# RMS norm factors by columns: two float32r matmuls with ones, root and reciprocal behind them, in a one-core decoder layer

## The chip, the cores and the metric

The kernel runs on one core of one Trainium2 chip. The metric is the device time of one execution in microseconds (us). The kernel before was timed three times. One further execution was taken with the hardware profiler; all rows of the profile come from that execution, and their times count from the start of its span.

The core has five engines with queues of their own that run in order: TensorE (PE in the profile, its weight loads are PEld), VectorE (DVE), ScalarE (ACT), GpSimd (POOL) and SyncE (SP), which issues most transfers. `te`, `ve`, `se` and `ge` stand for the first four in the code. PSUM has 8 banks of 128 x 512 float32 here, which take the results of matmuls.

## The reference

One layer of a decoder over 1024 prompt tokens and 8 x 4 decode tokens, model width 1024, in float32. Cut to what matters:

```
def _rms(x, g):
    return x * rsqrt(mean(x * x, axis=-1) + EPS) * g

h = _rms(x, n_mix_pre);  z = h @ w_in              # q, k, v, pooling input u
m = concat(attention(q, k, v), pool(u)) @ w_out
x = x + _rms(m, n_mix_post)
f = _rms(x, n_ffn_pre)
f = (silu(f @ w_gate) * (f @ w_up)) @ w_down
x = x + _rms(f, n_ffn_post)
x = x + sigmoid(x @ w_ple_gate) * (p @ w_ple)
```

The attention has 8 query heads on 2 key heads of 64, a window of 128 keys, and a learned sink for each head. The decode tokens attend to a cache of 128 keys for each of 8 sequences and to their own 4 keys. There are four norms on the way of every token.

## The kernel before

**Layout.** Activations are kept with channels on the 128 partitions and tokens along the columns. The 1056 tokens are cut into three groups of 352 columns (`G`, `N`); group 2 holds the last prompt tokens and the decode tokens. A matrix product of float32 is made of three float32r matmuls: each operand is split into a rounded part `hi` (a cast on ACT) and the rest `lo` (a subtraction on DVE, lines 157 and 160 in `split`), and `gemm` issues hi x hi, hi x lo and lo x hi. Nearly all of PE's work is matmuls of 128x128 weights with 352 columns, recorded at one line (126, in the helper `mm`).

**Stages.** In order of the span: the pooling input's projections with the first norm (to about 57 us), keys, values and queries (to about 135), the decode and prompt attention mixed with parts of the output projection (136 to 240), the rest of the output projection with the norms around the residual (240 to 285), the FFN (285 to 1010; group 2 goes ahead with five slabs of the hidden dimension alone, and groups 0 and 1 share products by sums of weights that POOL makes), and the per-layer input with its gate (to the end).

**The norms.** A norm's sum runs over channels, which lie on partitions and in eight column blocks. The blocks' squares are first added into one tile `acc` of 128 x 352 (`sum_halves`, `squares_into`). `rstd_steps(acc)` then makes the factor 1/sqrt(mean + eps) for each token. It is called twelve times: once for each group in front of the projections (`u_norm`, whose factor is used by `u_evict` and when keys, values and queries leave PSUM), twice for each group in `ffn_steps` (the norm behind the mixing, consumer line 834, and that in front of the FFN, line 846), and once for each group in `ple_steps` (consumer line 1050). Before, the four quarters of `acc`, 88 tokens each, are the stationary side of four narrow float32 matmuls with a column of ones; this gives sums with tokens on 88 partitions and four columns. Root (line 295), reciprocal (296) and split (298, 299) run on that 88x4 tile. Two products with the identity (line 303) spread the two parts over diagonals `dg`, and two float32r matmuls of ones with `dg` bring the factor back to all 128 partitions, in PSUM, where the consumers read it.

**What sets the order.** PE's instructions are pinned to the order of the program. Those of DVE and ACT are placed by a scheduler. `chain` and `turn` are a planner for the side work: a chain is a generator that yields (load, wait), in units of one 352-column matmul; `turn(n)` adds n units of PE time after a product and runs the chains whose time has come, where the time grows by load over a share (0.6, later 0.45, 0.1 and 0.7) plus the wait. So the two numbers that `rstd_steps` yields set how many matmuls of other work are between its two halves. For the three norms in front the two halves are placed by hand, with `u_norm`.

**The weights.** They are loaded by SP three tiles ahead and split when the program comes to them, so casts (ACT) and subtractions (DVE) of weights stand in the same queues as the norms.

**Decode attention.** `dscores(kv)` makes scores of 128 rows by 1056 keys for one key head, in three matmuls whose two operands lie on one half of the partitions (64 rows), adds the mask (line 688) and calls `softmax` (lines 589 to 603, the last step on POOL). `dturned` transposes the result block by block into a tile, and `dvalues(kv, pt, o)` multiplies nine blocks with the cached values, into one half of the output's partitions (64 columns of weights). Each of the nine matmuls takes all 128 columns, although for one cached sequence only 16 of them are not zero.

**The end.** `ple_out` makes two products for one block of channels and one group: `pp` from the per-layer input (2 blocks deep, 6 matmuls) and `pg` for the gate (8 deep, 24 matmuls), then sigmoid, multiplication, addition and the store.

Of the kernel before, what the change touches and what calls it, by code (L numbers as in the profile page):

```python
# [25 lines left out]
N = T // G  # L26
# [4 lines left out]
TB = 4  # L31
# [30 lines left out]
def trunk_kernel(  # L62
# [32 lines left out]
    te, ve, se, ge = nc.tensor, nc.vector, nc.scalar, nc.gpsimd  # L95
# [4 lines left out]
    spool = ctx.enter_context(tc.tile_pool(name="spool", bufs=2))  # L100
# [23 lines left out]
    def mm(*args, **kw):  # L124

        ins = te.matmul(*args, **kw)  # L126
        if pinned[0]:
            tc.keep_in_program_order(ins)

    def bank():  # L130
        return psum.tile([P, 512], F32, tag="b", name=nm("b"))

    def tmp(n, s="t", dt=F32):
        return spool.tile([P, n], dt, tag="tmp", bufs=6, name=nm(s), padded_shape=[P, NX])
# [21 lines left out]
    def split(hi, lo, src):  # L156
        ins = se.copy(hi, src)  # L157
        if not pairs:
            tc.keep_in_program_order(ins)
        ve.tensor_tensor(lo, src, hi.bitcast(F32), op=ALU.subtract)  # L160
# [124 lines left out]
    def rstd_steps(acc):  # L285

        n = acc.shape[1]
        w = n // TB  # L290
        sm = bank()
        for i in range(TB):
            mm(sm[:w, i : i + 1], acc[:, i * w : (i + 1) * w], ones[:, 0:1], start=True, stop=True)
        sd = spool.tile([P, TB], F32, tag="sd", name=nm("sd"))
        se.activation(sd[:w], sm[:w, :TB], AF.Sqrt, bias=epst[:w], scale=1.0 / D)
        ve.reciprocal(sd[:w], sd[:w])
        hl = spool.tile([P, 2, TB], F32R, tag="hl", name=nm("hl"))
        ve.tensor_copy(hl[:w, 0], sd[:w])
        ve.tensor_tensor(hl[:w, 1], sd[:w], hl[:w, 0].bitcast(F32), op=ALU.subtract)
        dgs = []  # L300
        for h in range(2):
            dg = tmp(n, "dg", F32R)
            ve.tensor_tensor(
                dg[:w].rearrange("p (i k) -> p i k", k=w),
                ident[:w, :w].unsqueeze(1).to_broadcast([w, TB, w]),
                hl[:w, h].bitcast(F32).unsqueeze(2).to_broadcast([w, TB, w]),
                op=ALU.mult,
            )
            dgs.append(dg)
        yield 6, 14  # L310
        ps = bank()
        for h in range(2):
            mm(ps[:, :n], ones_r[:w, :], dgs[h][:w], start=h == 0, stop=h == 1)
        return ps[:, :n]

    def acc_tile(g):
        return spool.tile([P, NS[g]], F32, tag=f"acc{g}", bufs=1, name=nm("acc"))
# [32 lines left out]
    xs, acc1, r1 = [[None] * 2 for _ in range(G)], [None] * G, [None] * G  # L350
# [51 lines left out]
    n = 4 * NDEC * PST  # L402
# [44 lines left out]
    def u_norm(steps, g):  # L447
        try:
            next(steps)
        except StopIteration as e:  # L450
            se.copy(acc1[g], e.value)
            r1[g] = acc1[g]

    pinned[0] = True
    norms = [None] * G
# [70 lines left out]
    for i, j in enumerate([WK, WV, *WQ]):  # L526
        w = weights(j)
# [3 lines left out]
        for g in range(G):  # L531
            ps = bank()
# [6 lines left out]
    kT, vT, qT = qkv[0], qkv[1], qkv[2:]  # L539
# [12 lines left out]
    skp, skd = const([P, 8], sink_p), const([P, 2], sink_d)  # L552
    nskp, nskd = const([P, 8]), const([P, 2])
# [32 lines left out]
    def softmax(t, nh, scale, sk, nsk):  # L586

        mx = spool.tile([P, nh], F32, tag="mx", name=nm("mx"))
        ve.tensor_reduce(mx, t, axis=AX.X, op=ALU.max)  # L589
        nmx = spool.tile([P, nh], F32, tag="nmx", name=nm("nmx"))  # L590
        ve.scalar_tensor_tensor(nmx, mx, -scale, nsk, op0=ALU.mult, op1=ALU.min)
        es = spool.tile([P, nh], F32, tag="es", name=nm("es"))
        ve.tensor_tensor(es, sk, nmx, op=ALU.add)
        se.activation(es, es, AF.Exp)
        sm = spool.tile([P, nh], F32, tag="sm", name=nm("sm"))
        for c in range(nh):
            se.activation(  # L597
                t[:, c, :], t[:, c, :], AF.Exp, bias=nmx[:, c : c + 1], scale=scale, accum_out=sm[:, c : c + 1]
            )
        ve.tensor_tensor(sm, sm, es, op=ALU.add)  # L600
        ve.reciprocal(sm, sm)
        nk = t.shape[2]
        ge.tensor_tensor(t, t, sm.unsqueeze(2).to_broadcast([P, nh, nk]), op=ALU.mult)  # L603
# [70 lines left out]
    nc.sync.dma_start(dmt, dmask)  # L674
    NK = NDEC * WIN + NDEC * DSEQ

    def dscores(kv):
        rows = slice(64 * kv, 64 * kv + 64)
        q = qd[rows]
        t = act_tile([P, 1, NK])  # L680
        for lo, n in ((0, 512), (512, 512), (1024, NDEC * DSEQ)):
            ps = bank()
            if lo < 1024:
                k = ckt[rows].rearrange("p b w -> p (b w)")[:, lo : lo + n]
            else:
                k = kT[rows, SEQ:]
            mm(ps[:, :n], q, k, start=True, stop=True)
            ve.tensor_tensor(t[:, 0, lo : lo + n], ps[:, :n], dmt[:, lo : lo + n], op=ALU.add)
        softmax(t, 1, 0.125, skd[:, kv : kv + 1], nskd[:, kv : kv + 1])
        return t  # L690

    def dturned(t):
        pt = act_tile([P, NDEC + 1, P])
        for lo in (0, 4, 8):
            ps = bank()
            n = min(4, NDEC + 1 - lo)
            if lo < 8:
                for i in range(n):
                    mt(ps[:, i * P : (i + 1) * P], t[:, 0, (lo + i) * P : (lo + i + 1) * P])
                se.copy(pt[:, lo : lo + n, :], ps.rearrange("p (b c) -> p b c", c=P))  # L700
            else:
                mt(ps[: NDEC * DSEQ, :P], t[:, 0, 1024:])
                se.copy(pt[: NDEC * DSEQ, 8, :], ps[: NDEC * DSEQ, :P])
        return pt

    def dvalues(kv, pt, o):
        cols = slice(64 * kv, 64 * kv + 64)
        for b in range(NDEC):
            mm(o[cols, :P], cvt[:, b, cols], pt[:, b, :], start=b == 0, stop=False)
        mm(o[cols, :P], vdec[:, cols], pt[: NDEC * DSEQ, 8, :], start=False, stop=True)  # L710

    def out_pool(m, g):

# [47 lines left out]

    order = [5, 6, 7, 0, 1, 2, 3, 4]
    pinned[0] = True
    td = [dscores(kv) for kv in range(2)]
    t = scores(order[0])
    filler(2)
    od = bank()
    pt0 = dturned(td[0])
    filler(1)
    pt1 = dturned(td[1])  # L770
    dvalues(0, pt0, od)
    filler(1)
    dvalues(1, pt1, od)
    put(od, SEQ, NDEC * DSEQ)
    kse = act_tile([P, NDEC, WIN])
    ge.tensor_copy(kse[:, :, : WIN - DSEQ], ckt[:, :, DSEQ:])
# [4 lines left out]
    for a, b in zip(order, order[1:] + [None]):  # L781
# [5 lines left out]
        t = t2  # L787
# [300 lines left out]
    def ple_out(n, m, g):  # L1088
        ph, pl = pls[g]
        w = WPE[n][m]  # L1090
        wh, wl = need(w[0])
        cols = slice((m % 4) * P, (m % 4 + 1) * P)
        pp, pg = bank(), bank()
        gemm(pp[:, :N], [(wh[:, k, cols], wl[:, k, cols], ph[:, k, :], pl[:, k, :]) for k in range(2)])
        gemm(pg[:, :N], ops8(need(w[1]), x2s[g]))
        turn(30)
        sg = tmp(N, "sg")
        se.activation(sg, pg[:, :N], AF.Sigmoid)
        xm = x2[g][m // 4][:, m % 4, :]
        ve.tensor_tensor(sg, sg, pp[:, :N], op=ALU.mult)  # L1100
        yo = tmp(N, "yo")
        ve.tensor_tensor(yo, sg, xm, op=ALU.add)
        nc.sync.dma_start(y_o[:, m, OFF[g] : OFF[g + 1]], yo)
# [105 lines left out]
```

## Time and profile before

| | |
|---|---|
| time, median of 3 runs | 1135.78 us (1133.85 to 1135.8) |
| the profiled execution's own time | 1133.7 us |
| its span | 1131.9 us |
| its granted TensorE clock, mean | 0.998 |
| PE busy | 1119.0 us (99%) |
| DVE, ACT, POOL busy | 745.5, 440.4, 176.0 us |
| read from memory, written | 88.30 MB, 10.11 MB |

How to read it: a group's row names line, engine, operation, output <- inputs, partitions x elements and count, then busy time, mean ns of one, and the idle time of the engine just ahead with what ended it. A row of the timeline gives start and duration, and in brackets the idle time ahead and what ended it. Neighbours of one kind are put into one row with a count. PE's matmuls overlap in its pipeline: one of 352 columns lasts some 323 ns in the records, and the next starts 160 ns after it.

### The profile page before, as it was taken

The page shows a single profiled execution, that of the slowest core. Times are in us where ns is not written, and L with a number is a line of the kernel's source. Part 1 is how long each engine was busy: PE and PEld are TensorE (multiplying, and loading weights), DVE is VectorE, ACT ScalarE, POOL GpSimd, SP SyncE. Part 2 cuts the span into 40 slices and gives each one's busy share as a digit, 9 for nine tenths or more (in the row PEclk, how much of TensorE's full clock was granted, in tenths as well). Part 3 has the DMA queues.
Part 4 walks back from the last instruction along what each step waited for, and adds up shares of the span by engine and source line. Part 5 has one row for each costly group of instructions (what it writes and reads, how often), then busy time and mean ns, then how long its engine had stood idle before and what let it go on. Part 6 is the DMA issues. An engine that isn't in the chain of part 4 may idle for free.

```text
span 1131.9 us, 17571 instructions
## 1 busy us (share of the span) xinstructions
PE 1119.0 (99%) x7119; PEld 1096.0 (97%) x7119; DVE 745.5 (66%) x1234; ACT 440.4 (39%) x772; POOL 176.0 (16%) x149
## 2 busy tenths in 40 slices
PE   8999999999999999999999999999999999999998
PEld 8999988699999999999999999999999999999998
DVE  7567357876888965256555555557887876789532
ACT  8223266754555533332221313123434334366220
POOL 0045032200000032111110201111123123100000
PEclk9999999999999999999999999999999999999999
DMA  8121301172454312112020211211322222256211
GB/s 285 49 77 39 126 37 38 39 268 85 172 192 131 112 56 75 38 39 75 25 70 19 75 38 41 73 38 60 119 73 76 75 75 75 85 172 213 89 59 39
DMA packets 34689, 99.54 MB, mean 88 GB/s; under 512 B 4116, under 2 KB 14644, under 8 KB 34608
## 3 DMA queue, kind: packets, MB, share of 16 engines
q1 hardware_dynamic: 32848, 96.65, 25.5%
q10 hardware_dynamic: 1760, 1.78, 0.5%
q8 instruction: 56, 0.92, 0.3%
q14 instruction: 25, 0.20, 0.1%
HBM read 88.30 MB, written 10.11 MB: 87 GB/s over the span
## 4 chain that ended last, share of the span: by engine, by line
PE 90%; DVE 5%; ACT 3%; issue 1%; DMA 1%; POOL 1%; DVEq 0%; POOLq 0%; ACTq 0%
PE b L126 89%; ACT a L597 1%; DVE mx L589 1%; DVE wl L160 1%; ACT wh L157 1%; PE b L120 1%; DMA wr<-in_w_in_dram 1%; POOL wr L923 0%; DVE a L634 0%; DVE h L360 0%; ACT h L357 0%; DMA c<-in_gains_dram 0%; DVE o L1050 0%; DVE x L1054 0%; POOL a L603 0%
## 5 line engine op out<-in xcount | busy, mean ns | idle before, releaser
L126 PE MATMUL b<-fh,wh 128*128 128x352 f32 x808 | 260.6, 323 | 0.0
L126 PE MATMUL b<-fh,wl 128*128 128x352 f32 x808 | 260.6, 323 | 0.0
L126 PE MATMUL b<-fl,wh 128*128 128x352 f32 x808 | 259.5, 321 | 0.0
L126 PE MATMUL b<-hid,wh 128*128 128x352 f32 x1056 | 253.6, 322 | 1.7 <-DVE o L1050 1.2
L157 ACT CAST wh<-wr 128x1024 fp32r<-128x1024 f32 x137 | 143.5, 1049 | 263.5 <-PE b L126 227.5
L160 DVE TENSOR_TENSOR wl<-wr,wh 128x1024 fp32r<-128x1024 f32 x137 | 171.2, 1252 | 64.6 <-ACT wh L157 64.3
L126 PEld LDWEIGHTS b<-hid,wh 128*128 128x128 f32 x1056 | 183.5, 188 | 2.5 <-issue 1.5
L126 PE MATMUL b<-hid,wl 128*128 128x352 f32 x528 | 170.1, 322 | 0.0
L923 POOL TENSOR_TENSOR wr<-wr 128x512 f32<-128x512 f32 x44 | 63.5, 1443 | 630.5 <-DVE wl L160 454.6
L126 PEld LDWEIGHTS b<-fh,wl 128*128 128x128 f32 x808 | 152.9, 189 | 0.0
L126 PEld LDWEIGHTS b<-fl,wh 128*128 128x128 f32 x808 | 151.9, 188 | 0.0
L126 PEld LDWEIGHTS b<-fh,wh 128*128 128x128 f32 x808 | 151.5, 188 | 0.0
L1020 DVE TENSOR_TENSOR o<-o,b 128x352 f32<-128x352 f32 x240 | 114.6, 515 | 27.4 <-PE b L126 27.0
L126 PE MATMUL b<-fh,sh 128*128 128x352 f32 x352 | 113.6, 323 | 0.0
L126 PE MATMUL b<-fh,sl 128*128 128x352 f32 x352 | 113.4, 322 | 0.0
L126 PE MATMUL b<-fl,sh 128*128 128x352 f32 x352 | 113.0, 321 | 0.0
L126 PE MATMUL b<-h,wh 128*128 128x352 f32 x480 | 105.9, 326 | 1.4 <-ACT h L357 0.9
L160 DVE TENSOR_TENSOR sl<-wr,sh 128x1024 fp32r<-128x1024 f32 x44 | 53.8, 1222 | 75.1 <-ACT sh L157 75.1
L126 PEld LDWEIGHTS b<-hid,wl 128*128 128x128 f32 x528 | 99.8, 189 | 0.0
L157 ACT CAST sh<-wr 128x1024 fp32r<-128x1024 f32 x44 | 45.7, 1047 | 131.3 <-POOL wr L923 91.0
L126 PEld LDWEIGHTS b<-h,wh 128*128 128x128 f32 x480 | 82.3, 190 | 2.7 <-ACT h L357 1.4
L126 PEld LDWEIGHTS b<-fh,sl 128*128 128x128 f32 x352 | 66.5, 189 | 0.0
(150 smaller groups left out, 1594.9 us busy)
## 6 DMA issues: line engine op xcount, KB each, us to landing
wr<-in_w_gu_dram SPq DMA_DIRECT2D x64, 512.0 KB, 3.3
wr<-in_w_dn_dram SPq DMA_DIRECT2D x32, 512.0 KB, 3.4
wr<-in_w_pg_dram SPq DMA_DIRECT2D x14, 512.0 KB, 3.8
wr<-in_w_in_dram SPq DMA_DIRECT2D x10, 512.0 KB, 4.2
x<-in_x_dram SPq DMA_DIRECT2D x6, 704.0 KB, 11.1
x1d<-x SPq DMA_DIRECT2D x6, 704.0 KB, 3.6
x<-x1d SPq DMA_DIRECT2D x6, 704.0 KB, 5.8
out_y_dram<-yo SPq DMA_DIRECT2D x24, 176.0 KB, 1.8
```

The lines of the kernel that those rows point to most:

```text
L120: ins = te.transpose(out, src, ident)
L126: ins = te.matmul(*args, **kw)
L157: ins = se.copy(hi, src)
L160: ve.tensor_tensor(lo, src, hi.bitcast(F32), op=ALU.subtract)
L589: ve.tensor_reduce(mx, t, axis=AX.X, op=ALU.max)
L597: se.activation(t[:, c, :], t[:, c, :], AF.Exp, bias=nmx[:, c : c + 1], scale=scale, accum_out=sm[:, c : c + 1])
L923: ge.tensor_tensor(out, a, b, op=op)
L1020: ve.tensor_tensor(o, o, v, op=ALU.add)
```

## The change

It has three parts.

1. `rstd_steps`: the narrow matmuls, the root and reciprocal on 88x4, and the diagonals go. `acc` itself is split into two float32r tiles, `ah` and `al`, and two float32r matmuls with a 128x128 tile of ones give each token's sum on all partitions. Root and reciprocal are made there on 128x352, from PSUM into `acc` (in SBUF), which is the factor. The yield between the two halves becomes (4, 8) instead of (6, 14). `u_norm` no longer copies the factor out of PSUM.
2. Decode: `dscores` makes the scores of both key heads, alternating between them, and calls both softmaxes behind. `dvalues` makes both heads' values in one block: the new keys' matmul first, over all 128 columns, and then one matmul for each sequence and head, alternating, over the 16 columns (4 heads x 4 tokens) that belong to that sequence.
3. `ple_out`: the gate's product is issued first, its sigmoid next, and then the product of the per-layer input.

```
     def rstd_steps(acc):
         n = acc.shape[1]
-        w = n // TB
-        sm = bank()
-        for i in range(TB):
-            mm(sm[:w, i : i + 1], acc[:, i * w : (i + 1) * w], ones[:, 0:1], start=True, stop=True)
-        sd = spool.tile([P, TB], F32, tag="sd", name=nm("sd"))
-        se.activation(sd[:w], sm[:w, :TB], AF.Sqrt, bias=epst[:w], scale=1.0 / D)
-        ve.reciprocal(sd[:w], sd[:w])
...
-        for h in range(2):
-            dg = tmp(n, "dg", F32R)
-            ve.tensor_tensor(
...
-        yield 6, 14
+        hi, lo = tmp(n, "ah", F32R), tmp(n, "al", F32R)
+        split(hi, lo, acc)
+        yield 4, 8
         ps = bank()
-        for h in range(2):
-            mm(ps[:, :n], ones_r[:w, :], dgs[h][:w], start=h == 0, stop=h == 1)
-        return ps[:, :n]
+        mm(ps[:, :n], ones_r, hi, start=True, stop=False)
+        mm(ps[:, :n], ones_r, lo, start=False, stop=True)
+        se.activation(acc, ps[:, :n], AF.Sqrt, bias=epst, scale=1.0 / D)
+        ve.reciprocal(acc, acc)
+        return acc
...
         except StopIteration as e:
-            se.copy(acc1[g], e.value)
-            r1[g] = acc1[g]
+            r1[g] = e.value
...
-    def dscores(kv):
-        rows = slice(64 * kv, 64 * kv + 64)
...
+    def dscores():
+        ts = [act_tile([P, 1, NK]) for _ in range(2)]
         for lo, n in ((0, 512), (512, 512), (1024, NDEC * DSEQ)):
+            for kv in range(2):
+                rows = slice(64 * kv, 64 * kv + 64)
...
+                mm(ps[:, :n], qd[rows], k, start=True, stop=True)
+                ve.tensor_tensor(ts[kv][:, 0, lo : lo + n], ps[:, :n], dmt[:, lo : lo + n], op=ALU.add)
+        for kv in range(2):
+            softmax(ts[kv], 1, 0.125, skd[:, kv : kv + 1], nskd[:, kv : kv + 1])
+        return ts
...
-    def dvalues(kv, pt, o):
-        cols = slice(64 * kv, 64 * kv + 64)
+    def dvalues(pts, o):
+        sides = [slice(64 * kv, 64 * kv + 64) for kv in range(2)]
+        def own(a, b):
+            return a.rearrange("p (h r) -> p h r", h=4)[:, :, DSEQ * b : DSEQ * (b + 1)]
+        for pt, cols in zip(pts, sides):
+            mm(o[cols, :P], vdec[:, cols], pt[: NDEC * DSEQ, 8, :], start=True, stop=False)
         for b in range(NDEC):
-            mm(o[cols, :P], cvt[:, b, cols], pt[:, b, :], start=b == 0, stop=False)
-        mm(o[cols, :P], vdec[:, cols], pt[: NDEC * DSEQ, 8, :], start=False, stop=True)
+            for pt, cols in zip(pts, sides):
+                mm(own(o[cols, :P], b), cvt[:, b, cols], own(pt[:, b, :], b), start=False, stop=b == NDEC - 1)
...
-    td = [dscores(kv) for kv in range(2)]
+    td = dscores()
     t = scores(order[0])
     filler(2)
     od = bank()
-    pt0 = dturned(td[0])
+    pts = [dturned(td[0])]
     filler(1)
-    pt1 = dturned(td[1])
-    dvalues(0, pt0, od)
+    pts.append(dturned(td[1]))
     filler(1)
-    dvalues(1, pt1, od)
+    dvalues(pts, od)
...
-        gemm(pp[:, :N], [(wh[:, k, cols], wl[:, k, cols], ph[:, k, :], pl[:, k, :]) for k in range(2)])
         gemm(pg[:, :N], ops8(need(w[1]), x2s[g]))
-        turn(30)
         sg = tmp(N, "sg")
         se.activation(sg, pg[:, :N], AF.Sigmoid)
+        gemm(pp[:, :N], [(wh[:, k, cols], wl[:, k, cols], ph[:, k, :], pl[:, k, :]) for k in range(2)])
+        turn(30)
```

More of the change, by code (lines that the diff above doesn't have):

```diff
@@ L289, in rstd_steps @@
         n = acc.shape[1]
-        w = n // TB
-        sm = bank()
-        for i in range(TB):
-            mm(sm[:w, i : i + 1], acc[:, i * w : (i + 1) * w], ones[:, 0:1], start=True, stop=True)
-        sd = spool.tile([P, TB], F32, tag="sd", name=nm("sd"))
-        se.activation(sd[:w], sm[:w, :TB], AF.Sqrt, bias=epst[:w], scale=1.0 / D)
-        ve.reciprocal(sd[:w], sd[:w])
[L297 to L300, printed above, removed]
-        for h in range(2):
-            dg = tmp(n, "dg", F32R)
[L303 to L309, printed above, removed]
-        yield 6, 14
-        ps = bank()
-        for h in range(2):
-            mm(ps[:, :n], ones_r[:w, :], dgs[h][:w], start=h == 0, stop=h == 1)
-        return ps[:, :n]
+        hi, lo = tmp(n, "ah", F32R), tmp(n, "al", F32R)
+        split(hi, lo, acc)
+        yield 4, 8
+        ps = bank()
+        mm(ps[:, :n], ones_r, hi, start=True, stop=False)
[3 more added lines that the diff above has]
+        return acc
     def acc_tile(g):
@@ L675, in trunk_kernel @@
     NK = NDEC * WIN + NDEC * DSEQ
-    def dscores(kv):
-        rows = slice(64 * kv, 64 * kv + 64)
-        q = qd[rows]
-        t = act_tile([P, 1, NK])
+    def dscores():
+        ts = [act_tile([P, 1, NK]) for _ in range(2)]
         for lo, n in ((0, 512), (512, 512), (1024, NDEC * DSEQ)):
[L682 to L690, printed above, removed]
+            for kv in range(2):
+                rows = slice(64 * kv, 64 * kv + 64)
+                ps = bank()
+                if lo < 1024:
+                    k = ckt[rows].rearrange("p b w -> p (b w)")[:, lo : lo + n]
+                else:
+                    k = kT[rows, SEQ:]
+                mm(ps[:, :n], qd[rows], k, start=True, stop=True)
[3 more added lines that the diff above has]
+        return ts
     def dturned(t):
```

## The prediction

> **What bounds the kernel now.** I read the busy times first, then the chain of work that ended last, then the list of what TensorE (PE) waited for, then stage windows, and last the timelines around the places that the change touches.
>
> ```profile
> span 1131.9 us, 17571 instructions
> PE 1119.0 (99%) x7119; PEld 1096.0 (97%) x7119; DVE 745.5 (66%) x1234; ACT 440.4 (39%) x772; POOL 176.0 (16%) x149
> PE 90%; DVE 5%; ACT 3%; issue 1%; DMA 1%; POOL 1%; DVEq 0%; POOLq 0%; ACTq 0%
> ...
> PE b L126 <- DVE dg L303: 2.0, 2, 1.6
> PE b L126 <- DVE o L1050: 1.2, 1, 1.2
> PE b L126 <- DVE hid L160: 0.5, 1, 0.5
> ...
> 300.00:420.00 120.00, 120.00 (x761) 119.96 (x760) 102.00 (x135) 60.69 (x74) 8.44 (x4) 1.00 0.41 139
> ```
>
> PE is busy for 99% of the span and is 90% of the chain that ended last. The waits row reads "PE waited for DVE's tile dg 2.0 us in all, 2 times, at most 1.6". In the window from 300 to 420 us (columns: length, then PE, weight loads, DVE, ACT and POOL busy with their counts, clock, DMA share, GB/s) PE has no idle time and the clock is 1.00. So what counts is the work on PE itself, to the last tenth of a microsecond, and whatever makes PE wait that did not before. DVE's 66% and ACT's 39% are cover, except where they sit between two PE instructions.
>
> **Part 1: the norm without its turn to columns.** Twelve norms run through the changed helper: one for each of 3 groups ahead of the projections, two for each in the mixing and FFN norms, one for each before the per-layer input.
>
> ```profile
> 24.77 0.71 PE L126 MATMUL b<-c,acc 128*88 128x1 f32 x8
> ...
> 26.71 0.80 PE L126 MATMUL b<-h,wl 128*128 128x352 f32 x4
> 29.11 0.78 PE L126 MATMUL b<-dg,c 88*128 88x352 f32 x2 [1.60 <-DVE dg L303]
> 31.65 1.44 PE L126 MATMUL b<-h,wh 128*128 128x352 f32 x8
> 32.93 0.81 PE L126 MATMUL b<-h,wl 128*128 128x352 f32 x4
> ...
> L126 PE MATMUL b<-c,acc 128*88 128x1 f32 x96 | 8.5, 211 | 0.0
> L126 PE MATMUL b<-dg,c 88*128 88x352 f32 x24 | 6.4, 344 | 2.2 <-DVE dg L303 2.0
> ```
>
> The 96 passes of the four narrow float32 matmuls (8 a norm) go. Rows overlap in PE's pipeline, so I take the spacing, not the duration: with them, from the start of the passes to the start of the next 4 matmuls of the same block is 26.71 - 24.77 = 1.94 us; the same block without them takes 32.93 - 31.65 = 1.28. That is 0.66 a norm, 12 x 0.66 = **-7.9 us** of PE work. The two wide matmuls stay: 24 before, with the diagonals dg, 24 after, with the squares' halves as the moving side. Same 352 columns, same type, so I count no difference.
>
> The first norm makes PE wait 1.60 us for dg. Four matmuls in a row take 0.81 (at 32.93), each alone 0.32, so the next could start 0.16 after the last: 26.71 + 4 x 0.16 = 27.35. The dg matmuls start at 29.11, 1.76 later, and the two take 0.78 where two in a row take 0.48, another 0.30: the place cost 2.06 above normal. After the change only a cast and a subtraction stand between acc and the wide matmuls, and acc was there before 24.77, while PE comes at about 26.7. **-2.06 us.**
>
> ```profile
> L157 ACT CAST hid<-sl 128x352 fp32r<-128x352 f32 x22 | 10.6, 484 | 39.3 <-DVE sl L974 39.3
> L160 DVE TENSOR_TENSOR hid<-sl,hid 128x352 fp32r<-128x352 f32 x22 | 11.5, 521 | 7.2 <-ACT hid L157 7.2
> L728 ACT ACTIVATE sq<-b 128x352 f32<-128x352 f32 x12 | 5.4, 454 | 0.0
> L601 DVE RECIPROCAL sm<-sm 128x4 f32<-128x4 f32 x16 | 2.8, 173 | 0.3
> L601 DVE RECIPROCAL sm<-sm 128x1 f32<-128x1 f32 x2 | 0.3, 164 | 0.1
> L295 ACT ACT_TABLE_LOAD x6 | 7.7, 1283 | 0.1
> ...
> 1014.83 0.43 PE L126 MATMUL b<-dg,c 88*128 88x352 f32 x1
> 1015.70 0.43 PE L126 MATMUL b<-dg,c 88*128 88x352 f32 x1 [0.44 <-DVE dg L303]
> ```
>
> At the second place, the norm of group 0 before the per-layer input, the second dg matmul started 0.87 after the first (a row apart: 0.16) and waited 0.44 of it; with the first's own delay I put the loss at 1.1. The narrow matmuls' yields shrink from 6 and 14 to 4 and 8 planner units, so this matmul now comes six wide matmuls earlier (1.0) and without the narrow ones (0.7), about 1013.1; a cast of 0.48 and a subtraction of 0.52 behind the last square leave it waiting some 0.8 instead: I take **-0.3** (ends -1.1 and +1).
>
> What is added per norm: the cast (0.484) and the subtraction (0.521) before the wide matmuls, and **behind** them a root of 128x352 out of PSUM (nearest row: the square, 0.454) and a reciprocal of 128x352. Gone from DVE are the two wide dg, the 88x4 reciprocal, cast and subtraction, five operations for two. ACT gets 0.484 + 0.454 a norm, 11 us in all, less its 88x4 root. Both have cover where PE runs alone. But before, the matmul's result was the finished factor; now two operations more lie between PE and every consumer. The reciprocal's price no row shows at this width. From below: its step from 1 to 4 elements, 173 - 164 = 9 ns, is 3 ns an element, with a rounding error that allows 1 ns (0.164 + 0.35 = 0.5 us); from above, at 4.7 ns (14 ns), 1.8 us. I take 0.5, as the subtraction of that width costs 0.52, and keep 1.8.
>
> [...]
>
> Where that longer tail reaches PE is the start of the FFN.
>
> ```profile
> 273.74 1.07 DVE L846 SCALAR_TENSOR_TENSOR y<-x,c,b 128x352 f32<-128x352 f32 x2 [2.04 <-PE b L126]
> 274.66 0.45 ACT L728 ACTIVATE sq<-b 128x352 f32<-128x352 f32 x1
> 284.41 1.63 DVE L160 TENSOR_TENSOR fl<-y,fh 128x1408 fp32r<-128x1408 f32 x1
> 285.06 0.32 PE L126 MATMUL b<-fh,wh 128*128 128x352 f32 x1
> 287.14 0.32 PE L126 MATMUL b<-fl,wh 128*128 128x352 f32 x1
> ```
>
> DVE is released by PE at 273.74, works without a pause to the second half of the FFN's operand (284.41 + 1.63 = 286.04), and PE uses that half at 287.14: 1.1 us in hand. After: the root stands on ACT behind a weight cast and this square, so it ends about 275.1 + 0.45, the reciprocal at 276.1 to 276.4 with its semaphores, which is 2.4 to 2.7 later than 273.74; and the next norm's subtraction (0.52), which the planner brings forward, is put in the same DVE queue ahead of the half. 286.04 + 2.7 + 0.5 = 289.3 against 287.14: PE stands for **+2.2 us** (ends 0, if the scheduler's filler overlaps, and 4.5). Queued behind the reciprocal on DVE are the weight splits that PE needs, so a later one would also be paid there. The other norms show no wait for dg in the row above (two waits in twelve), so a factor some 1 to 2 us later is hidden by the projections or the FFN's products in front of it.
>
> ```profile
> 827.84 3.15 DVE L1054 SCALAR_TENSOR_TENSOR x<-o,c,x 128x352 f32<-128x352 f32 x2
> 832.58 0.43 PE L126 MATMUL b<-hid,wh 128*128 128x352 f32 x1 [0.51 <-DVE hid L160]
> 878.56 1.61 DVE L1050 TENSOR_TENSOR o<-o,b 128x1408 f32<-128x1408 f32 x1
> 880.32 0.56 PE L126 MATMUL b<-hid,wh 128*128 128x352 f32 x2 [1.22 <-DVE o L1050]
> ```
>
> Two waits in the FFN come from group 2's last norm: two products of 1.6 us each hold DVE at 827.84, and the scaling of the FFN's output at 878.56 stands ahead of what frees hid. With other yields and a factor in SBUF these land elsewhere in DVE's order; the listing of the changed program has the scaling behind the eight additions that PE waits for. I take **-2.0** (ends -2.0 and 0): 0.5 + 1.2 and the pipeline's restart. The root's table loads (1.28 each, two more) and the smaller SyncE moves (the residual's stores, later weight loads) lie on queues that PE doesn't wait for; if that cover failed, two loads cost 2.6.
>
> **Part 2: decode.** The scores' six matmuls alternate the two row halves, the values' 18 become 36 of which 32 have 16 columns, alternating the column halves.
>
> ```profile
> 137.75 2.22 DVE L688 TENSOR_TENSOR a<-b,a 128x512 f32<-128x512 f32 x4
> 139.88 1.24 DVE L589 TENSOR_REDUCE mx<-a 128x1 f32<-128x1056 f32 x1
> ...
> 144.00 1.95 POOL L603 TENSOR_TENSOR a<-a,sm 128x1056 f32<-128x1056 f32 x1 [7.52 <-DVE sm L601]
> 146.01 1.20 PE L120 MATMUL b<-c,a 128*128 128x128 f32 x9 [0.43 <-POOL a L603]
> 150.06 2.32 PE L126 MATMUL b<-a,a 128*64 128x128 f32 x18
> 154.41 4.30 PE L126 MATMUL b<-a,a 128*64 128x128 f32 x50
> 163.56 0.19 PEld L126 LDWEIGHTS b<-a,a 128*64 128x64 f32 x2 [0.22 <-ACT a L597]
> ```
>
> PE's scores shorten by up to 1 us, but softmax is now issued for both halves behind all six additions, and both reduces stand ahead of the first sum: two more additions (2.22 / 4 = 0.56 each) and one more reduce, 2.3 us. So POOL's first normalisation, at 144.00 before, comes some 2.3 later, and PE's transposes with it (146.01 to about 148.3, with 3.9 us idle in front, against 0.43). Then the values: before, 18 passes from 150.06 (2.24) and 18 of the 50 from 154.41 (2.24), ending 156.66; after, one block that waits for the second half's transposes (about 155.2) and takes 1.8 to 2.9. It ends near 157.0: **+0.3** (ends -1.5 and +3.3).
>
> The two loads at 163.56 of the prompt's values, for the two column halves, begin as a pair in 0.19. [...]
>
> **Part 3: the tail.**
>
> ```profile
> 1127.49 0.46 ACT L1098 ACTIVATE sg<-b 128x352 f32<-128x352 f32 x1 [4.34 <-PE b L126]
> 1127.99 0.52 DVE L1100 TENSOR_TENSOR sg<-sg,b 128x352 f32<-128x352 f32 x1 [3.72 <-ACT sg L1098]
> ```
>
> With the gate first, the last sigmoid runs beside the six matmuls of the other product; DVE's multiplication follows PE at once: 1127.99 - 1127.49 = **-0.5**. Elsewhere PE hides it.
>
> Sum: -7.9 - 2.06 - 0.3 - 2.0 + 2.2 + 0.3 - 0.5 = **-10.3**. The profiled execution's own time is 1133.7 (span 1131.9), 2.1 below the median of 1135.78; from the median, 1125.5.
>
> **The rivals.**
> - R2, the FFN starts without a stall, because the scheduler puts the split ahead: 1125.5 - 2.2 = 1123.3. For it: DVE loses the two dg; against it: DVE had no gap after 273.74.
> [...]
> - R4, decode loses its upper end, since TensorE stands while both softmaxes are run: 1125.5 + 3.0 = 1128.5. For it: POOL's start hangs on DVE's order.
> - R5, slower: the root and reciprocal, with a table load in front (1.28 + 0.45 + 0.5 = 2.2), hold in-order DVE behind PE at each of the nine later norms, and the weight and hidden splits behind it arrive late: 9 x 2.2 = 19.8 instead of my +2.2: 1125.5 + 17.6 = 1143. It decides from about 1.4 us passed on at each (12.5/9). For it: the waits at 832.58 and 880.32 show that one late DVE operation reaches PE. Against it: both were 1.6 us operations ahead of hid, and ten of twelve norms had no wait.
> - R6, it doesn't do what it says: the narrow passes ran beside other matmuls, and PE's spacing stays: 1133 to 1136. Against it: the 0.66 is spacing, not duration.
>
> **How the numbers follow.** My forecast 0.42, R2 0.20, R3 0.14, R4 0.10, R5 0.10, R6 0.04. What a measurement can tell from no change is 0.2%, 2.3 us. Faster: 0.42 + 0.20 + 0.14 + 0.10 = 0.86; same 0.04; slower 0.10. The forecast's own bounds (-2.2 FFN, -1.8 decode; +2.3, +2.0) make 1121 to 1130; R2 with the lower ends gives 1120, R3 and R4 together 1131. I give 1120 to 1131, and leave out R5 and R6.
>
> **What would show it.** The group of 96 narrow passes is gone and PE's busy time falls by about 8. No wait for dg; in its place one for fl at the FFN's start, near 280, of 1 to 4 us. [...] In decode an idle PE ahead of the transposes. The prediction is wrong if a wait for a weight split or hid, repeated by norm, appears beside the reciprocal.

## The result and the profile after

The changed kernel takes 1152.95 us (median of 6 runs, 1146.34 to 1153.89) against 1134.82 for the kernel before beside it: ratio 1.0148, 95% interval 1.0122 to 1.0174. It is slower by some 17 us, where 10 us less were forecast. The profiled execution has a span of 1148.0 us against 1131.9, so the traces differ by 16.1.

The page of the changed kernel: span, busy times, and the chain that ended last by engine.

```profile
span 1148.0 us, 17363 instructions
PE 1118.9 (97%) x7023; PEld 1094.7 (95%) x7023; DVE 765.3 (67%) x1198; ACT 449.7 (39%) x783; POOL 174.2 (15%) x149
...
PE 84%; DVE 8%; issue 2%; ACT 2%; POOL 2%; DMA 1%; DVEq 0%; SPq 0%; POOLq 0%; ACTq 0%
```

PE runs 96 instructions fewer, yet is busy for as long, and stands idle for 3% of the span. What it waited for, in the view of TensorE's waits (total, times, longest):

```profile
PE b L126 <- ACT hid L157: 8.4, 3, 4.6
PE b L120 <- POOL a L585: 3.2, 1, 3.2
PE b L126 <- DVE fl L160: 2.8, 2, 1.6
PE b L126 <- ACT fh L157: 2.7, 2, 1.5
PE b L126 <- DVE hid L160: 2.0, 3, 1.1
PE b L126 <- DVE al L160: 1.2, 2, 1.0
```

These six rows are 20.3 us, 21.0 with what is left for o (0.7); the rows of before that answer to them (dg, o, hid and a, in the prediction) are 4.1. The waits for hid, fh and fl are operands of the FFN and of the last stage. The two new operations of the norm, from the groups by line and shape:

```profile
L296 DVE RECIPROCAL acc<-acc 128x352 f32<-128x352 f32 x12 | 28.2, 2350 | 2.9 <-ACT acc L295 2.9
L295 ACT ACTIVATE acc<-b,c 128x352 f32<-128x352 f32 x12 | 6.6, 554 | 0.9 <-PE b L126 0.9
```

The reciprocal of 128x352 takes 2.35 us: (2350 - 164) / 351 = 6.2 ns an element, where the step of the two narrow rows gave 3. The root takes 0.55.

**The FFN's start**, timeline of PE and, first, of DVE:

```profile
269.55 2.35 DVE L296 RECIPROCAL acc<-acc 128x352 f32<-128x352 f32 x1
...
278.70 0.32 PE L126 MATMUL b<-fh,wh 128*128 128x352 f32 x1
...
282.28 0.42 PE L126 MATMUL b<-fh,wh 128*128 128x352 f32 x1 [1.50 <-ACT fh L157]
284.26 0.43 PE L126 MATMUL b<-fl,wh 128*128 128x352 f32 x1 [1.56 <-DVE fl L160]
...
285.64 0.49 PE L126 MATMUL b<-fh,wl 128*128 128x352 f32 x1
285.94 0.49 PE L126 MATMUL b<-fh,wh 128*128 128x352 f32 x1
```

PE comes to the FFN 6.4 us ahead of the kernel before: its first matmul there starts at 278.70, where the prediction's row has 285.06. So the change's savings are there at this point, and are lost behind it. Two waits of 1.50 and 1.56 follow; then, from 285.35 to 288.8, matmuls start 0.29 apart where 0.16 is usual. Nothing is waited for there: PE itself is slow. That is 1.6 us on top of the waits. The pipeline's start behind the two waits is another 0.5: the matmuls there last 0.42 and 0.43 us, where 0.32 is usual, and the one behind the second starts 0.27 on (284.53), where 0.16 is usual. Windows inside the slow stretches at the four large waits show it as the granted clock (the column after POOL's):

```profile
285.30:288.60 3.30, 3.30 (x14) 3.30 (x13) 0.76 (x1) 1.82 (x2) 0.00 (x0) 0.50 0.00 0
316.00:319.30 3.30, 3.30 (x13) 3.30 (x12) 3.30 (x4) 1.75 (x2) 0.00 (x0) 0.50 0.78 280
845.10:848.40 3.30, 3.30 (x13) 3.30 (x12) 1.71 (x4) 0.00 (x0) 0.00 (x0) 0.50 0.10 41
1073.80:1077.10 3.30, 3.30 (x14) 3.30 (x13) 0.99 (x1) 1.41 (x2) 0.00 (x0) 0.50 0.15 55
```

13 or 14 matmuls run in 3.3 us, where 20 are usual. The clock is at 0.50 for 3.4 us at three of the places, and near 312 us for 6.8 us, which begin while PE still waits. At the FFN's start two waits of 3.06 us together, with one matmul between, went ahead of it.

**Near 312 us**, and **near 843 us**, rows of several engines' timelines:

```profile
301.36 2.35 DVE L296 RECIPROCAL acc<-acc 128x352 f32<-128x352 f32 x1
...
307.77 3.16 DVE L824 TENSOR_TENSOR x<-x,y 128x1408 f32<-128x1408 f32 x2
309.42 1.38 ACT L825 ACTIVATE y<-x 128x1408 f32<-128x1408 f32 x1 [4.25 <-DVE x L824]
310.84 0.52 DVE L963 TENSOR_TENSOR sl<-sl,b 128x352 f32<-128x352 f32 x1
310.96 1.38 ACT L825 ACTIVATE y<-x 128x1408 f32<-128x1408 f32 x1 [0.16 <-DVE x L824]
312.24 0.47 ACT L157 CAST hid<-sl 128x352 fp32r<-128x352 f32 x1
312.76 0.66 PE L126 MATMUL b<-hid,wh 128*128 128x352 f32 x1 [4.61 <-ACT hid L157]
...
834.47 1.45 POOL L912 TENSOR_TENSOR wr<-wr 128x512 f32<-128x512 f32 x1 [17.06 <-DVE wl L160]
839.27 0.51 DVE L946 TENSOR_TENSOR p<-p,b 128x352 f32<-128x352 f32 x1
840.53 1.04 ACT L157 CAST sh<-wr 128x1024 fp32r<-128x1024 f32 x1 [5.24 <-POOL wr L912]
841.48 0.49 ACT L989 ACTIVATE p<-p 128x352 f32<-128x352 f32 x1
843.30 0.48 ACT L157 CAST hid<-u 128x352 fp32r<-128x352 f32 x1 [1.33 <-DVE u L990]
843.84 0.43 PE L126 MATMUL b<-hid,wh 128*128 128x352 f32 x1 [3.57 <-ACT hid L157]
```

In the first, ACT waits 4.25 us for the norm's additions on DVE, squares two halves, and only then casts hid, which PE has been waiting for. The cast's input sl is made on DVE behind the same additions: it starts at 310.84, though PE, which makes one of its factors, stands idle from 308.15 and the other left ACT at 305.16. It ends at 311.36, and the cast begins at 312.24, behind the second square. Both queues went in order here, so the norm's late additions and squares hold an operand of the FFN that has nothing to do with them. (PE also comes to this product 2.6 us earlier than before, at 307.51 against 310.07.)

In the second, two casts stand in another order on ACT. Now the cast of POOL's sums (`sh`) waits 5.24 us for POOL. The silu ahead of hid's cast, whose input was there at 839.78, starts only behind it, at 841.48, and hid's cast at 843.30. In the kernel before, hid's cast went first:

```profile
827.96 0.49 ACT L157 CAST hid<-u 128x352 fp32r<-128x352 f32 x1 [1.80 <-DVE u L1001]
832.18 1.05 ACT L157 CAST sh<-wr 128x1024 fp32r<-128x1024 f32 x1 [3.73 <-POOL wr L923]
```

POOL's sums are not late by themselves. They start 8.4 us later than before (834.47 against 826.09), but PE, too, is some 8 us behind the kernel before at this point.

At the last stage PE waits 1.24 and 1.23 us for fh and fl near 1071.

### The profile page after: what moved, and what is told of

The parts are those of the page before. It is cut to its first block, busy times and chain, and to the rows that moved or that the text cites. A ratio compares the mean times of both kernels' runs of the same rounds, so it can differ in the third digit from the quotient of the medians.

```text
span 1148.0 us, 17363 instructions
## 1 busy us (share of the span) xinstructions
PE 1118.9 (97%) x7023; PEld 1094.7 (95%) x7023; DVE 765.3 (67%) x1198; ACT 449.7 (39%) x783; POOL 174.2 (15%) x149
## 4 chain that ended last, share of the span: by engine, by line
PE 84%; DVE 8%; issue 2%; ACT 2%; POOL 2%; DMA 1%; DVEq 0%; SPq 0%; POOLq 0%; ACTq 0%
PE b L126 84%; DVE wl L160 2%; POOL wr L912 1%; ACT a L579 1%; DVE mx L571 1%; DVE a L616 1%; PE b L120 0%; DVE x L1043 0%; ACT wh L157 0%; DMA wr<-in_w_gu_dram 0%; DVE fl L160 0%; DVE acc L719 0%; DMA pr<-in_p_dram 0%; DVE sl L160 0%; DMA wr<-in_w_in_dram 0%
## 5 line engine op out<-in xcount | busy, mean ns | idle before, releaser
L126 PE MATMUL b<-hid,wh 128*128 128x352 f32 x1056 | 257.9, 326 | 11.1 <-ACT hid L157 8.4
L126 PEld LDWEIGHTS b<-hid,wh 128*128 128x128 f32 x1056 | 187.1, 191 | 13.2 <-ACT hid L157 9.3
L912 POOL TENSOR_TENSOR wr<-wr 128x512 f32<-128x512 f32 x44 | 60.4, 1373 | 650.4 <-DVE wl L160 648.6
L126 PEld LDWEIGHTS b<-fl,sh 128*128 128x128 f32 x352 | 66.6, 189 | 0.0
```

Source lines behind the costliest of these rows:

```text
L912: ge.tensor_tensor(out, a, b, op=op)
```

## The experiments

All ratios are to the kernel before on the same chip, with their 95% intervals; where one run was taken, its time is given.

| run | what it is | ratio |
|---|---|---|
| e1 | norm's part alone | 1.0133 (1.0103 to 1.0164) |
| e2 | decode part alone | 1.0010 (1.0000 to 1.0020) |
| e3 | end alone | 1.0002 (0.9992 to 1.0012) |
| e4 | change, multiplication for reciprocal | 0.9992 (0.9965 to 1.0019) |
| e5 | change, yields 6 and 14 | 1.0108 (1.0092 to 1.0124) |
| e6 | change, inverse root on ScalarE | 0.9997 (0.9982 to 1.0012) |
| e7 | before, new norm in the first three | 0.9978 (0.9968 to 0.9987) |
| e9 | change, old norm in the last three | 1.0066 (1.0046 to 1.0085) |
| e10 | change, old norm in six of the FFN's | 1.0067 (1.0053 to 1.0081) |
| e11 | before, new decode values | 1.0001 (0.9992 to 1.0010) |
| e12 | first three norms, values, end | 1.0001 (0.9992 to 1.0010) |

The theories: T1, the wide reciprocal on in-order DVE; T2, the shorter yields; T3, the decode part; T4, the slow clock behind pauses; T5, one delay at the FFN's start that is handed on.

**Each part alone (e1 to e3).** The diffs are those of the change, one part each.

> The kernel before with the norm's part of the change alone (no decode part, no change of the end). T1 (the reciprocal of 128x352, 2.35 us on DVE, and the work that it makes late in the in-order queues of DVE and ACT is the loss): the whole loss and a little more, 15 to 20 us slower than before, with waits for fh and fl at the FFN's start, for hid near 310 and 840 us and for fh and fl near 1070, each wait of 2.5 us or more followed by some 3.4 us of matmuls at a lower clock. T3 (the decode part is a main cause): at most 13 us slower.

> The kernel before with the decode part alone. T3 (decode is a main cause, since TensorE waits 3.2 us for POOL's normalisation ahead of the transposes): 2 to 4 us slower. T1: no loss, since the shorter scores and values give that wait back: between 1.5 us faster and 0.5 us slower, with the wait of about 3 us there all the same.

> The kernel before with the gate's product first in the last stage, and nothing else. All theories: 0.3 to 0.6 us faster at the end of the span, which is within the runs' scatter; the last sigmoid is done before the last matmul ends.

The norm's part alone is 15 us slower, all of the loss within the intervals; its trace has the expected waits, but for one of 2.9 us near 1052 in the place of those near 1070. Decode costs 1.1 us (0 to 2.3), between what T1 and T3 expected; PE waits 3.2 for POOL there. A slow clock behind that wait (some 2 us) is in e2's trace and in the second one of the whole change (e15), not in its first. The end alone is within the scatter. T3 falls as a main cause.

**The reciprocal's price (e4, e6).**

```
-        ve.reciprocal(acc, acc)
+        ve.tensor_scalar(acc, acc, 1.0, None, op0=ALU.mult)      # e4
...
-        se.activation(acc, ps[:, :n], AF.Sqrt, bias=epst, scale=1.0 / D)
-        ve.reciprocal(acc, acc)
+        se.activation(acc, ps[:, :n], AF.Abs_reciprocal_sqrt, bias=epst, scale=1.0 / D)   # e6
```

> The changed kernel with a multiplication by 1.0 of the same 128x352 tile in the place of the reciprocal, so that the root is used where its inverse belongs; this leaves the inverse out. T1 (the reciprocal's price): the multiplication takes about 0.5 us, 12 x 1.85 us of DVE go, and the kernel is 2 to 10 us faster than before: of the waits, those near 1070 and at the FFN's start go down to about 1 us each or vanish, and with them the lower clock. T2 (the shorter yields of 4 and 8 bunch the norms' side work): the wait of 4.6 us for hid near 310 stays, and the kernel is no more than 2 us faster than before, or slower.

> The changed kernel with one activation on ScalarE (the inverse root of the absolute value) in the place of root and reciprocal: nothing of the norm stands on VectorE behind the matmul. It keeps the computation but for that function's rounding. T1: 18 us or more of the loss go, as with the multiplication, and the kernel is 2 to 8 us faster than before; the waits near 1070 and at the FFN's start are at most 1 us each. If the price is not the reciprocal but the place of two more operations behind the matmul, no more than half of the loss goes.

e4 leaves the inverse out. From the groups by line, e4 and then e6:

```profile
L296 DVE TENSOR_SCALAR acc<-acc 128x352 f32<-128x352 f32 x12 | 4.1, 339 | 2.3 <-ACT acc L295 2.3
```

```profile
L295 ACT ACTIVATE acc<-b,c 128x352 f32<-128x352 f32 x12 | 6.7, 555 | 0.1
```

With 0.34 instead of 2.35 us, 1.0148 - 0.9992 = 1.6% or 17.7 us come back; with nothing on DVE, 17 us. The traces are 20.1 and 12.2 us shorter than the change's. Part of that is the matmuls' spacing, which differs between these executions (last runs below); at the change's spacing it would be some 14 and 15 us, an estimate from the counts of matmuls in windows. So the length of the reciprocal, on an engine that is busy for 67% of the span, is most of the loss: the waits at the FFN's start, near 312 and near 1071, 11.2 us together in the change, are 3.2 in e4 and 2.0 in e6.

But neither is clearly faster than before, against the 2 us and more of T1. PE still waits for hid near 305 us (0.84 and 1.33 in e4, 0.21 and 1.32 in e6) and near 830 (3.3 and 0.65 in e4, 4.7 in e6), and 3.2 in decode, with a slow stretch behind several of them. Those waits are not the reciprocal's. The one near 830 is the change's wait near 843, and comes from the order of the two casts on ACT, here in e6:

```profile
831.16 1.04 ACT L157 CAST sh<-wr 128x1024 fp32r<-128x1024 f32 x1 [6.28 <-POOL wr L911]
...
833.93 0.48 ACT L157 CAST hid<-u 128x352 fp32r<-128x352 f32 x1 [0.94 <-DVE u L989]
```

e4 has the same order. A scheduler sets it, so the kernels differ in more than the one operation.

**The yields (e5).**

```
-        yield 4, 8
+        yield 6, 14
```

> The changed kernel with the norm's two yields put back to 6 and 14. T1 (the reciprocal's 2.35 us in the in-order queue): little comes back, 2 to 5 us at the most, and the kernel stays 12 us or more slower than before. T2 (the shorter yields bunch the side work of groups 0 and 1): the wait of 4.6 us for hid near 310 us goes and with it the slow clock behind it, 6 to 8 us come back, about 10 us slower than before.

4.5 us come back (1.0148 - 1.0108), and the kernel stays 12 us slower than before. The wait of 4.6 for hid near 313 us is 3.3 and not gone, and the slow clock behind it stays. T1's figure holds. T2 is a minor part at most: e15, the change once more with the spacing of matmuls that e5 has, spans 1144.5 us against e5's 1142.1, so some 2 us are left for the yields by these two traces.

**Which of the later norms (e9, e10).** The helper of before, with its yields of 6 and 14, stands beside the new one and is called at these places:

```
-        r = yield from rstd_steps(acc3[g])
+        r = yield from rstd_narrow(acc3[g])        # e9: the last three
...
-        r = yield from rstd_steps(acc[g])
+        r = yield from rstd_narrow(acc[g])         # e10, and the same for acc2
```

> The changed kernel with the old norm in the three norms ahead of the per-layer input, the new one in the other nine. T1 (each late norm pays at its own place): the waits near 840 and 1070 us and the slow clock behind them go (some 12 us), three old norms' narrow matmuls and the waits of the kernel before come back (some 4 us): 7 to 11 us slower than before. T5 (the delay at the FFN's start is handed on through the weight splits to all later places): the waits near 840 and 1070 stay, 13 us or more slower.

> The changed kernel with the old norm in the six norms between attention and FFN, the new one in the first three and the last three. T1: the waits at the FFN's start and near 312 us and the slow clock behind them go (some 13 us), six times 0.66 us come back: 6 to 11 us slower than before, with the waits near 840 and 1070 in place. T5: those go too, and the kernel is no slower than before.

Two windows of each kernel (length, PE busy and its count, weight loads, DVE, ACT, POOL, clock, DMA share, GB/s): before, the change, e9, e10.

```profile
280.00:320.00 40.00, 40.00 (x260) 39.96 (x259) 34.79 (x42) 25.51 (x36) 0.00 (x0) 1.00 0.55 191
820.00:850.00 30.00, 29.49 (x184) 29.04 (x183) 26.34 (x39) 8.53 (x11) 7.64 (x6) 1.00 0.22 71
```

```profile
280.00:320.00 40.00, 31.24 (x165) 30.05 (x165) 33.10 (x31) 21.69 (x26) 0.00 (x0) 0.87 0.48 175
820.00:850.00 30.00, 25.27 (x143) 24.21 (x142) 24.87 (x35) 12.63 (x18) 5.79 (x4) 0.94 0.27 88
```

```profile
280.00:320.00 40.00, 31.09 (x163) 29.98 (x162) 31.95 (x31) 21.63 (x26) 0.00 (x0) 0.86 0.44 153
820.00:850.00 30.00, 29.49 (x184) 29.04 (x184) 26.98 (x42) 10.27 (x15) 5.82 (x4) 1.00 0.26 88
```

```profile
280.00:320.00 40.00, 40.00 (x260) 39.93 (x260) 34.79 (x40) 25.23 (x36) 0.00 (x0) 1.00 0.58 198
820.00:850.00 30.00, 25.29 (x137) 24.11 (x136) 22.91 (x36) 6.43 (x9) 5.79 (x4) 0.89 0.21 71
```

Each place heals where the old norm is put back and only there: 9.3 us come back by the one, 9.2 by the other. Near 830, e9 has the two casts of ACT in the order of before (hid at 833.00, `sh` at 837.22), e10 in that of the change (835.84 and 833.07). T5 falls; the losses are local and add up (9.3 + 9.2, less the 2.5 that e7 wins, plus 1.1 for decode, is 17.1, against 16.8 for the ratio 1.0148).

**A pause by itself (e8).** In the kernel before, after one slab each:

```
+    def pause(k):
+        b1, b2 = bank(), bank()
+        mm(b1[:, :P], ones_r, ones_r, start=True, stop=True)
+        se.copy(scr[:, :P], b1[:, :P])
+        for _ in range(k):                       # 2, 5, 8, 11
+            ge.tensor_scalar(scr, scr, 1.0, None, op0=ALU.mult)
+        mm(b2[:, :P], ones, scr[:, :P], start=True, stop=True)
```

> The kernel before with four pauses of TensorE in the FFN, made by a chain of 2, 5, 8 and 11 small GpSimd operations between two small extra matmuls after one slab each; nothing else is changed. T4 (a pause costs more than its length, since the matmuls behind it run at a lower clock for some 3.4 us): behind the pauses of 3 us and more the spacing of matmuls is 0.29 instead of 0.16 us for a while, 1.9 to 2.3 us lost each beside the pause, the same for the longest; behind the shortest one nothing. Against T4: the spacing stays 0.16 behind all four, and the slow stretches in the changed kernel are of another origin.

```profile
514.46 0.49 PE L127 MATMUL b<-c,c 128*128 128x128 f32 x2 [1.59 <-POOL c L463]
...
515.27 0.33 PE L127 MATMUL b<-fh,wh 128*128 128x352 f32 x1
...
585.29 0.79 PE L127 MATMUL b<-c,c 128*128 128x128 f32 x2 [4.56 <-POOL c L463]
...
587.35 0.49 PE L127 MATMUL b<-fh,wl 128*128 128x352 f32 x1
```

Behind 1.59 us nothing; behind 4.56, 6.41 and 8.23 the matmuls are 0.29 apart for a while, 2.0, 2.4 and 1.5 us lost. The time was 1164.3 us. T4 holds: the three longer pauses cost their length and about 2 us more, with no growth from 4.56 to 8.23. (The first norm's wait was 3.2 us in this execution, against 1.6 in the first, and had 1.6 us of slow matmuls behind it.) Where the cost begins these pauses do not show: behind waits of 1.9 us (the first norm in e2, whose mean granted clock was 0.994, against 0.998 before) and 1.7 us (e11, below, 0.50) the clock fell too.

**What gains (e7, e11, e12).** e7's label names the end too, but its kernel has only the three norms.

```
-    norms[0] = rstd_steps(acc1[0])
+    norms[0] = rstd_wide(acc1[0])        # e7: and [1], [2]; rstd_wide is the new helper
...
-    dvalues(0, pt0, od)
...
-    dvalues(1, pt1, od)
+    dvalues(pts, od)                     # e11: the new one, behind both halves' transposes
```

> The kernel before with the new norm for the three norms ahead of the projections alone, the old one for the other nine; old decode, old end. T1: these three have consumers that TensorE does not wait for, so the narrow matmuls (3 x 0.66) and the first wait (2.06) are won: 3 to 5 us faster than before, with no new wait behind 240 us. If the wide reciprocal costs wherever it stands: no gain, or a wait of TensorE between 29 and 57 us.

> The kernel before with the decode values as in the change (36 matmuls that alternate the column halves, most of 16 columns) and the scores and softmax as before. If the values win 2.6 us and the order of the softmax loses 2.8: the wait for POOL's normalisation stays at 0.4 us, and the kernel is 1 to 3 us faster than before; less, if the waits for the prompt's softmax between 190 and 225 us take the gain up. If the alternation itself is dear: no gain.

> The parts that seem to gain, together: the new norm for the first three norms, the new decode values with the old scores and softmax, and the gate's product first at the end; old norm in the other nine. By T1 the gains add up: 5 to 8 us faster than before, with no wait behind 240 us that the kernel before doesn't have. If the attention's softmax chain takes up what the values gain: 3 to 5 us.

e7 is the one kernel that beats both, by 2.5 us, a little less than expected. Its trace has no new wait, and at 220 us it stands 4.4 us ahead of before (the prompt's softmax wait is at 219.94 against 224.37); then it loses 3.5 of it between 308 and 820 us without waiting for anything. e11's values are shorter, but PE now waits 1.7 us for the copies of the second half's transposes, and behind this wait the clock is low:

```profile
154.40:161.10 6.70, 6.70 (x69) 6.44 (x69) 0.74 (x2) 1.33 (x3) 1.25 (x3) 0.50 0.22 81
```

The values and scores behind the wait take 5.97 us there, where a like group of the change, at the full clock, takes 3.90. So nothing is won. e12 has that wait too, without the slow clock, and no gain either: its matmuls are further apart than those of before in the FFN and behind it (715 against 726 between 885 and 1000 us), which by an estimate from such counts takes some 6 us.

**Second profiles (e13, e14, e15)**, of before, of e7's kernel and of the change, all unchanged.

> The kernel before once more, unchanged, for a second profile. T6 (the spacing of the matmuls takes one of three values, 158.9, 160.0 or 161.1 ns, settled anew by each pause, and which one is chance): between 360 and 790 us, where the first profile had 160.0, another value is as likely. T7 (the value belongs to the program): 160.0 again in that stretch.

> The kernel before with the new norm in the first three norms alone, once more, for a second profile. The first had 161.1 ns between 308 and 820 us, which takes 3.5 us of the 4.4 that it had won at 220 us. T6: another value is as likely, and at 158.9 the span is about 7 us shorter than in the first profile. T7: 161.1 again, and the same span within 1 us.

> The changed kernel once more, for a second profile. T6: its span differs from the first by up to 7 us, with another spacing between 384 and 828 us (161.1 in the first), and the waits of the first profile stand at the same places. T7: 161.1 again in that stretch. Either way the waits near 282, 313, 843 and 1070 us are there, each with slow matmuls behind it where it is 2.5 us or more.

They took 1133.45, 1132.83 and 1146.31 us. Windows of PE alone: before, e14, the change's first profile, its second (e15).

```profile
430.00:630.00 200.00, 200.00 (x1252) 1.00 0.16 50
```

```profile
430.00:630.00 200.00, 200.00 (x1243) 1.00 0.15 52
```

```profile
430.00:630.00 200.00, 200.00 (x1243) 1.00 0.15 48
```

```profile
430.00:630.00 200.00, 200.00 (x1261) 1.00 0.14 48
```

PE is full and the clock is 1.00 in all four, and yet 1243, 1252 or 1261 matmuls fit into 200 us: mean spacings of 161.1, 160.0 and 158.9 ns (two of each count straddle the ends of the window). The changed kernel had the slowest in one execution and the fastest in the other (3.5 us of span); before and e7's kernel had the same value in both (T7). In e8 the spacing settles anew behind every pause: 160.0, then 161.1, 160.0, 161.1 and 158.9. So in these executions the value is set again by a pause, and the two programs without pauses there keep theirs. That is e7's lost 3.5 us, and it fits a part of the changed kernel's scatter. What selects the value stays open.

## Why the prediction was wrong

The step that failed is the price of the reciprocal, with the step that followed from it: "a factor some 1 to 2 us later is hidden by the projections or the FFN's products in front of it". I took 0.5 us and kept 1.8 as the upper end; it measured 2.35. The rows of 1 and 4 elements behind both ends are too small to give a slope: their step of 3 ns an element makes 1.2 us, and 6.2 was measured; the 0.5 leaned on the subtraction's price alone. R3's 0.14 and the 2.5 us by which it lifts R4's 1128.5 to the 1131 at the upper end stand for a dearer reciprocal, and no run shows that term: the runs showed 2.35 us, and a loss well above 2.5, since the late factor was priced at one place only, the FFN's start. In place of a hidden delay the runs showed 11.2 us of waits at the FFN's start, near 312 and near 1071, of which 2 to 3 are left without the reciprocal; a wait of PE near 843 from the order of ACT's queue; and the lower clock behind the waits, which no term had.

R5 had the right mechanism and sign, with a chance of 0.10: late weight and hidden operands behind DVE. Its price of 2.2 us was made of a table load (1.28) and a reciprocal of 0.5, and is near the measured 2.9 of root and reciprocal (0.55 + 2.35) by luck; its 1143 is 10 us below the measured 1152.95.

Point by point:
- Narrow matmuls, -7.9: the 96 are gone, and nothing took their place on PE. The gain is there, under a larger loss.
- First place, -2.06: right. PE goes through without a stop:

```profile
25.88 0.81 PE L126 MATMUL b<-h,wl 128*128 128x352 f32 x4
26.53 0.32 PE L126 MATMUL b<-ah,c 128*128 128x352 f32 x1
26.69 0.32 PE L126 MATMUL b<-al,c 128*128 128x352 f32 x1
26.85 1.45 PE L126 MATMUL b<-h,wh 128*128 128x352 f32 x8
```

- Second place, a wait of 0.8 for al: measured 0.99 near 1027 us. Right in kind and size.
- FFN's start, +2.2: two waits of 3.06 together, 1.6 of slow clock and 0.5 for the pipeline's start, 5.1 in all. The mechanism was right, the size off by the reciprocal and by the clock, which no term had.
- Late waits, -2.0: wrong in sign. That place has 4.7 us of waits and 1.6 of slow clock, since hid's cast now stands behind the cast of POOL's sums.
- The waits near 312 and 1071 us were in no term. I had priced the norm where its own result is used, and not where ACT's and DVE's queues carry something else that PE needs.
- Decode, +0.3: e2 is 1.1 us slower, inside the ends. The wait came (3.2, forecast 3.9). The values take 149.91 to 151.75, 1.8 us, the lower end. I read their number wrongly: there are 18 matmuls before and after, each recorded as two passes, so 36 rows in both; what falls is the columns, from 128 to 16 in 32 of them. This group of 32 (row below) keeps PE busy for 1.1 us: two passes, taken here as one of each column half, start every 58 ns, where one pass of 128 columns took 109 before. The loads of such a pair start 6 ns apart and last 0.14 us each, and all 32 lie between 150.71 and 151.72: in this trace the loads of the two column halves overlap.

```profile
L126 PE MATMUL b<-a,a 128*64 128x16 f32 x32 | 1.1, 210 | 0.0
```

- Tail, -0.5: the span ends 4.1 us behind the last matmul's end, 4.4 before; e3 can't tell it from nothing.

An account of the 16.1 us between the traces: waits +16.6 (all rows of the waits view but the warm-up's, 23.7 against 7.1), slow clock and the pipeline's start behind waits +8.5 (spacing above 160 ns around the slow stretches, 7.0 of it at clock 0.50), spacing of 161.1 over 444 us +3.1, narrow matmuls -7.9, shorter decode scores and values -3.2, end -0.4: 16.7. What stays open is why the scheduler puts the sums' cast ahead of hid's with the new norm, and what makes the waits near 305 us that remain without the reciprocal (e4, e6): the order of ACT's and DVE's queues was not varied by itself.

## What to carry to other kernels

An operation that moves from a narrow tile to a wide one needs a price at the wide shape (the reciprocal here: 0.17 us at 88x4, 2.35 at 128x352), and its place in the engine's queue can matter more than its consumer, as near 312 us: ask for every instance what stands behind it on that engine, and on the engines that wait for that one. Compare the order of those queues before and after, too, where a scheduler sets it. On an engine that is full, allow for the clock on top of a new wait: here 1.6 us were lost to it behind the two waits at the FFN's start (3.06 us together) and 1.5 to 2.4 behind each of e8's pauses of 4.56 us and more. Before a difference of a few us is put down to an edit, compare the spacing of the matmuls in a stretch without waits. Use the wide form where nothing in the queue behind it is urgent, as in e7's three places, and keep the narrow one elsewhere.

## What the runs showed of the hardware

- The wide reciprocal on DVE took 2.35 us for 128x352, 6.2 ns an element; a multiplication of the same tile 0.34 (e4); the inverse root on ACT 0.55, from PSUM (e6).
- The granted clock was 0.50 for 3.4 or 6.8 us around and behind pauses of PE: at every pause of 3.3 us and more here, and at two waits in a row of 1.50 and 1.56 us and of 1.24 and 1.23 us. Single waits of 1.7 (e11) and 1.9 us (e2) had it, others of 1.6 (before, e8) and 1.7 us (e12) did not; the wait of 3.2 us in decode had it in some executions and not in others.
- Back-to-back matmuls of 352 columns settled at 158.9, 160.0 or 161.1 ns in the stretches without waits, and in e8 each pause settled them anew. Over some 500 us of the FFN that is an estimate of up to 7 us (500 x 2.2 / 160) without any wait or change of clock.
